# An encoder trunk on one core: SSD decay sums by triangle matmuls instead of scans over rows from DRAM, with a new interleaving

## The chip, the cores and the metric

The kernel runs on one core of one Trainium2 chip. The metric is the device time of one execution in microseconds; the time before is the median of three runs. The engines are TensorE (PE, with its weight loads PEld as a second track), VectorE (DVE), ScalarE (ACT), GpSimd (POOL) and SyncE (SP), which issues most DMAs and waits in order like the others.

## The reference

Two post-norm layers over 512 positions of width 1024. Each layer mixes with two head groups side by side and then runs an MLP:

```python
mix = concat([y_ssd, y_s5], -1) @ w_out
h = layer_norm(ALPHA * h + mix)
h = layer_norm(ALPHA * h + square(relu(h @ w1)) @ w2)
```

The SSD group has 16 heads, two directions and chunks of 128 positions. Its decay matrix, per head, direction and chunk, is what the change touches:

```python
Adt  = dt * A                               # one row of 512 per head and direction
Lmat = exp(_segsum(Adt))                    # exp of sums of Adt over (s, t], lower triangle
CB   = einsum('bclgn,bcsgn->bgcls', Cc, Bc)
y_diag = einsum('bgcls,bgrcls,bcsgrp->bclgrp', CB, Lmat, X)
```

The S5 group has 64 channel groups, each with a complex diagonal state, a forward and a backward scan, a gelu and a gated projection.

## The kernel before

All matrix products of weights are done as three fp32r matmuls (`mm3`: high part by high, high by low, low by high). For each weight tile, ACT writes the high part `whi` and DVE the low part `wlo`. Other products are plain fp32 and go through TensorE as two instructions each.

A layer is a mixer and an MLP. The mixer merges two generators. `ssd_group` runs for four groups; each has a convolution for B and for C, the products `cb_ps` with two masks (`CBU`, `CBLo`), and then two channel tiles of two heads each, 16 heads in all. `s5_stream` first makes the input states (tables `Wv`, matmuls `v_ps`), then 62 steps of a scan (three small DVE operations `sc`, `sc`, `cur` and an ACT copy each), then for m = 0 to 7 an output table `Wy` (DVE), its small products `kk_ps`, and the output matmuls `y` with `gT` transposes. In layer 0 the `Wv` and `Wy` tables are computed in the mixer; those of layer 1 are computed beforehand, during the MLP of layer 0 (`s5_tables`, drawn on by the string `gen`), and are loaded.

`KN["mrg"]` says how many S5 steps are drawn before each SSD step, `lag` how many tiles the input states trail, `po` which pieces get an offset in priority. The instructions' order on each engine is then set by a scheduler at build time. What is left of the S5 stream after the last SSD step is emitted ahead of the output projection of the SSD half (`rows_proj(A["wo"][l, 0], ...)`, matmuls `rp`), and the scheduler may mix the two. Then comes the gated projection `glu_ps`.

For one head, before: a DMA `ab` spreads two rows of Adt (one per direction, the first or last element of each chunk made -1e30 by two small operations in `dt_prep`) over 128 partitions. One scan adds along t and restarts at each chunk's diagonal by a maximum with the constant `md`; a second runs backward from the first's result; ACT takes the exponential:

```python
V.tensor_tensor_scan(E2, ab[:, 0], C("md"), NEG, op0=ALU.add, op1=ALU.max)
V.tensor_tensor_scan(E[:, ::-1], ab[:, 1][:, ::-1], E2[:, ::-1], NEG, op0=ALU.add, op1=ALU.max)
S.activation(E, E, AF.Exp)
```

The tile `ab` has one buffer, E has two. E is multiplied by the weighted mask products `w` and used in `y_ps` (L632); `eb` rows, also from DRAM, feed the terms between chunks (L635, L638). PSUM tags: `mm` three banks, `ss` one, `sm` two (`Xrow_ps`, `Brow_ps`, `cb_ps`, `st_ps`), `s5` two.

Of the kernel before, what the change touches and what calls it, by code (L numbers as in the profile page):

```python
# [10 lines left out]
F32 = mybir.dt.float32  # L11
F32R = mybir.dt.float32r
I32 = mybir.dt.int32
AF = mybir.ActivationFunctionType
# [27 lines left out]


KN = dict(
    mrg=[[5, 0, 1, 0, 3, 0, 3, 5, 0, 10, 1, 3, 0, 9, 4, 0, 0, 0, 1, 0,
# [3 lines left out]
    pt0=3, lag=[2, 5], vb=(3, 2), gvb=(3, 2), cbb=2, wyb=4, raw=2, whi=3, wlo=3,  # L49
    nb=dict(mm=3, ss=1, sm=2, s5=2),  # L50
    po=[{"dt": 60, "z": 30, "v": 60, "w": 150, "scan": 300}, {"w": -30, "dt": 150, "scan": 30}], curb=2,
    gen="112122220000021030201011",
)


# [1 line left out]
def kernel(ctx: ExitStack, tc: tile.TileContext, A, out, depth=L):  # L57
# [19 lines left out]
    def C(n):  # L77
        a, b = CST[n]
        return cst[:, a:b]
# [209 lines left out]
    def dt_prep(l, pool, hT, prm):  # L289
        wd = pool.tile([128, 8, 32], F32, tag="wd", name="wd", bufs=1)  # L290
        nc.sync.dma_start(wd, A["wd"][l])
        p = psum("sm", "dtp")
        for k in range(8):
            for i in range(2):
                for c in range(4):
                    PE.matmul(p[32 * c:32 * c + 32, 0:128], lhsT=wd[:, k],
                              rhs=hT[i][:, k, c * 128:(c + 1) * 128].bitcast(F32),
                              start=(k == 0 and i == 0), stop=(k == 7 and i == 1),
                              tile_position=(0, 32 * c))

        def t(nm, n=128):
            return pool.tile([128, n], F32, tag="dt_" + nm, name="dt_" + nm, bufs=1)
        v, e, z, z2, q, dt = t("v"), t("e"), t("z"), t("z2"), t("q"), t("dt")
        V.tensor_scalar(v, p[:, 0:128], prm["P"]("dtb"), None, op0=ALU.add)
        V.scalar_tensor_tensor(e, v, -1.0, v, op0=ALU.mult, op1=ALU.max)
        S.activation(e, e, AF.Exp, scale=-1.0)
        V.tensor_scalar(z, e, 2.0, None, op0=ALU.add)
        V.reciprocal(out=z, in_=z)
        V.tensor_tensor(z, z, e, op=ALU.mult)
        V.tensor_tensor(z2, z, z, op=ALU.mult)  # L310
        V.tensor_scalar(q, z2, 1.0 / 17, None, op0=ALU.mult)
        for c in (15, 13, 11, 9, 7, 5, 3):
            V.scalar_tensor_tensor(q, q, 1.0 / c, z2, op0=ALU.add, op1=ALU.mult)
        V.scalar_tensor_tensor(q, q, 1.0, z, op0=ALU.add, op1=ALU.mult)
        V.tensor_scalar(v, v, 0.0, None, op0=ALU.max)
        V.scalar_tensor_tensor(dt, q, 2.0, v, op0=ALU.mult, op1=ALU.add)
        aef = pool.tile([128, 2, 128], F32, tag="dt_aef", name="dt_aef", bufs=1)
        a, ef = aef[:, 0], aef[:, 1]
        V.tensor_scalar(a, dt, prm["A"], None, op0=ALU.mult)
        Pp, Rp, one = t("P", 129), t("R", 129), C("ones")  # L320
        V.memset(Pp[:, 0:1], 0.0)
        V.memset(Rp[:, 128:129], 0.0)
        V.tensor_tensor_scan(Pp[:, 1:129], one, a, 0.0, op0=ALU.mult, op1=ALU.add)
        V.tensor_tensor_scan(Rp[:, 0:128][:, ::-1], one, a[:, ::-1], 0.0, op0=ALU.mult, op1=ALU.add)
        dec, tot = z, t("tot", 1)
        isf, isb = C("isf"), C("isb")
        V.tensor_scalar(ef, Pp[:, 1:129], isf, None, op0=ALU.mult)
        V.scalar_tensor_tensor(ef, Rp[:, 0:128], isb, ef, op0=ALU.mult, op1=ALU.add)
        V.tensor_scalar(dec, Rp[:, 1:129], isf, None, op0=ALU.mult)
        V.scalar_tensor_tensor(dec, Pp[:, 0:128], isb, dec, op0=ALU.mult, op1=ALU.add)  # L330
        S.activation(ef, ef, AF.Exp)
        S.activation(dec, dec, AF.Exp)
        S.activation(tot, Pp[:, 128:129], AF.Exp)
        V.tensor_tensor(dec, dec, dt, op=ALU.mult)
        for i, c in ((0, isf), (127, isb)):
            V.tensor_scalar(a[:, i:i + 1], c, NEG, a[:, i:i + 1], op0=ALU.mult, op1=ALU.add)
        ad = dr.tile([2, 16, 2, 4, 128], F32, tag="ad", name="ad", bufs=2)
        for c in range(4):
            nc.sync.dma_start(ad[:, :, :, c].rearrange("d h i s -> (d h) i s"), aef[32 * c:32 * c + 32])
        p = psum("sm", "dtT")  # L340
        PE.transpose(p[:, 0:128], dt, ident)
        PE.transpose(p[:, 128:256], dec, ident)
        tb = q
        V.tensor_scalar(tb, one, tot, None, op0=ALU.mult)
        PE.matmul(p[:, 256:384], lhsT=tb, rhs=ident, start=True, stop=True)
        fac = per.tile([128, 3, 4, 2, 16], F32, tag="fac", name="fac", bufs=1)
        S.activation(fac.rearrange("p a c d h -> p (a c d h)"), p[:, 0:384], AF.Copy)
        return dict(ad=ad, dtT=fac[:, 0], dec=fac[:, 1], tot=fac[:, 2])


    def s5_u(us, o, Ud, m):
# [209 lines left out]
    def ssd_group(l, pool, act, prm, dtp, g, yd, ys):  # L561
# [16 lines left out]
        for j in range(2):  # L578
# [27 lines left out]
            for h in range(2):  # L606
                hh = 2 * ct + h
                E = pool.tile([128, T], F32, tag="E", name="E", bufs=2)
                E2 = pool.tile([128, T], F32, tag="tmp", name="E2", bufs=3)
                ab = pool.tile([128, 2, T], F32, tag="ab", name="ab", bufs=1)  # L610
                eb = pool.tile([128, 2, 384], F32, tag="eb", name="eb", bufs=2)
                nc.sync.dma_start(ab, dtp["ad"][:, hh, 0].rearrange("d c s -> d (c s)").unsqueeze(0).to_broadcast(
                    [128, 2, T]))
                for dd in range(2):
                    nc.sync.dma_start(eb[:, dd], dtp["ad"][dd, hh, 1, 1 - dd:4 - dd].rearrange(
                        "c s -> (c s)").unsqueeze(0).to_broadcast([128, 384]))
                V.tensor_tensor_scan(E2, ab[:, 0], C("md"), NEG, op0=ALU.add, op1=ALU.max)
                V.tensor_tensor_scan(E[:, ::-1], ab[:, 1][:, ::-1], E2[:, ::-1], NEG, op0=ALU.add, op1=ALU.max)
                S.activation(E, E, AF.Exp)
                w = pool.tile([128, 4, 128], F32, tag="w", name="w", bufs=1)  # L620
                w2 = pool.tile([128, 4, 128], F32, tag="tmp", name="w2", bufs=3)
                for c in range(4):
                    S.activation(w[:, c], CB[0][:, c], AF.Copy, scale=dtp["dtT"][:, c, 0, hh:hh + 1])
                    S.activation(w2[:, c], CB[1][:, c], AF.Copy, scale=dtp["dtT"][:, c, 1, hh:hh + 1])
                V.tensor_tensor(w, w, w2, op=ALU.add)
                Ev = E.rearrange("p (c n) -> p c n", c=4)
                V.tensor_tensor(Ev, Ev, w, op=ALU.mult)
                V.tensor_tensor(eb[:, 0], CT[:, 128:512], eb[:, 0], op=ALU.mult)
                V.tensor_tensor(eb[:, 1], CT[:, 0:384], eb[:, 1], op=ALU.mult)
                for c in range(4):  # L630
                    o = yp[64 * h:64 * h + 64, c * 128:(c + 1) * 128]
                    PE.matmul(o, lhsT=X[:, c, 64 * h:64 * h + 64], rhs=E[:, c * 128:(c + 1) * 128],  # L632
                              start=True, stop=False, tile_position=(0, 64 * h))
                    if c > 0:
                        PE.matmul(o, lhsT=St[0][:, c - 1, 64 * h:64 * h + 64], rhs=eb[:, 0, (c - 1) * 128:c * 128],  # L635
                                  start=False, stop=(c == 3), tile_position=(0, 64 * h))
                    if c < 3:
                        PE.matmul(o, lhsT=St[1][:, c, 64 * h:64 * h + 64], rhs=eb[:, 1, c * 128:(c + 1) * 128],  # L638
                                  start=False, stop=True, tile_position=(0, 64 * h))
                yield  # L640
# [304 lines left out]
def prepare(inp):  # L945
# [66 lines left out]
    cput("id", s == t)  # L1012
    cput("U", t >= s)
    cput("Lo", t <= s)
    cput("md", np.where(np.tile(t == s, (1, 4)), 0.0, 2 * NEG))
    cput("i16", (s % 16) == np.arange(16)[None])
    isf = ((s // 16) % 2 == 0)
    cput("isf", isf)
# [20 lines left out]
```

## Time and profile before

| | |
|---|---|
| median of the runs shown | 1901.4 us (1901.06 to 1903.05) |
| the profiled execution, its own time | 1897.68 us |
| its span | 1895.7 us |
| busy: PE, PEld, DVE, ACT, POOL | 1711.2, 1398.3, 1307.6, 778.1, 73.7 us |
| mean granted TensorE clock | 0.951 |
| DMA | 275.68 MB, mean 145 GB/s |

Busy times are unions over an engine's instructions; a busy PE counts a matmul's latency too. Layer 0's mixer takes about 60 to 537 us, its MLP up to about 1035, layer 1's mixer 1035 to 1430, its MLP the rest. The granted clock is told as a share of full speed (1.0 is 2.4 GHz, 0.5 is 1.2 GHz).

### The profile page before, as it was taken

The numbers are of one execution on the slowest core, as the hardware profiler recorded it, in microseconds if no ns is written. First come the engines' busy times: TensorE is split into PE (matmuls) and PEld (weight loads), VectorE is DVE, ScalarE is ACT, GpSimd is POOL, SyncE is SP. The second block draws the span as 40 slices with busy tenths as digits, with TensorE's granted clock in tenths as the row PEclk, the third lists the DMA queues.
The fourth block names the chain that finished last, engine by engine and source line by source line (L and its number), as shares of the span: only waits on it lengthen the run. The fifth ranks groups of instructions, "written<-read, shape, count | busy, mean of one in ns | idle before, by whom it ended". The sixth has DMA issues, their size and how long they took to land.

```text
span 1895.7 us, 27446 instructions
## 1 busy us (share of the span) xinstructions
PE 1711.2 (90%) x10872; PEld 1398.3 (74%) x10872; DVE 1307.6 (69%) x2176; ACT 778.1 (41%) x1305; POOL 73.7 (4%) x99
## 2 busy tenths in 40 slices
PE   4989888687799999999999999875989999999998
PEld 3767666575578877778888887665767888888886
DVE  7789989997646889994446679999614663434345
ACT  3356556742143433223233466657314332323231
POOL 1000000000000101110001000000000010000001
PEclk8999899788799999999999999887999999999999
DMA  5887444244324188763335784432683422333232
GB/s 191 238 217 200 114 116 138 73 156 117 103 98 133 62 263 278 260 217 108 101 123 168 228 263 130 123 100 73 207 236 123 126 75 89 101 98 96 83 101 89
DMA packets 120864, 275.68 MB, mean 145 GB/s; under 512 B 11424, under 2 KB 55456, under 8 KB 120096
## 3 DMA queue, kind: packets, MB, share of 16 engines
q1 hardware_dynamic: 113248, 247.85, 43.7%
q0 software_dynamic: 7488, 26.09, 3.7%
q8 instruction: 85, 1.39, 0.3%
q14 instruction: 43, 0.35, 0.1%
HBM read 237.06 MB, written 36.83 MB: 144 GB/s over the span
## 4 chain that ended last, share of the span: by engine, by line
PE 64%; DVE 19%; DMA 9%; issue 4%; ACT 4%; POOL 0%; POOLq 0%; SPq 0%; DVEq 0%; ACTq 0%
PE rp L105 8%; PE rp L106 8%; PE rp L104 8%; PE up_ps L104 5%; PE up_ps L105 5%; PE up_ps L106 5%; PE y L518 3%; DVE wlo L94 3%; DMA ab<-ad 2%; PE glu_ps L104 2%; PE glu_ps L105 2%; PE glu_ps L106 1%; PE xbc_ps L104 1%; DMA Bv<-in_bb 1%; PE xbc_ps L105 1%
## 5 line engine op out<-in xcount | busy, mean ns | idle before, releaser
L94 DVE TENSOR_TENSOR wlo<-raw,whi 128x1024 fp32r<-128x1024 f32 x224 | 273.4, 1221 | 302.0 <-ACT whi L93 298.4
L93 ACT ACTIVATE whi<-raw 128x1024 fp32r<-128x1024 f32 x224 | 237.4, 1060 | 511.0 <-PE up_ps L105 189.7
L104 PE MATMUL up_ps<-hThi,whi 128*128 128x512 f32 (+1 forms) x560 | 208.7, 375 | 3.3 <-DVE hr L907 3.0
L105 PE MATMUL up_ps<-hTlo,whi 128*128 128x512 f32 (+1 forms) x560 | 209.0, 374 | 0.1
L106 PE MATMUL up_ps<-hThi,wlo 128*128 128x512 f32 (+1 forms) x560 | 208.7, 373 | 0.0
L105 PE MATMUL rp<-wlo,ahi 128*128 128x512 f32 x448 | 176.8, 395 | 0.4 <-DVE wlo L94 0.4
L106 PE MATMUL rp<-whi,alo 128*128 128x512 f32 x448 | 176.6, 395 | 0.0
L104 PE MATMUL rp<-whi,ahi 128*128 128x512 f32 x448 | 165.5, 397 | 0.9 <-ACT whi L93 0.9
L104 PE MATMUL xbc_ps<-hThi,whi 128*128 128x512 f32 x256 | 106.6, 416 | 18.1 <-DVE xbc L548 14.6
L104 PEld LDWEIGHTS up_ps<-hThi,whi 128*128 128x128 f32 x560 | 105.4, 189 | 23.7 <-issue 2.2
L105 PEld LDWEIGHTS up_ps<-hTlo,whi 128*128 128x128 f32 x560 | 105.9, 189 | 18.9 <-issue 0.4
L106 PEld LDWEIGHTS up_ps<-hThi,wlo 128*128 128x128 f32 x560 | 105.8, 189 | 18.7 <-issue 0.2
L106 PE MATMUL xbc_ps<-hThi,wlo 128*128 128x512 f32 x256 | 104.3, 408 | 0.0
L105 PE MATMUL xbc_ps<-hTlo,whi 128*128 128x512 f32 x256 | 104.1, 407 | 0.0
L104 PEld LDWEIGHTS rp<-whi,ahi 128*128 128x128 f32 x448 | 83.9, 188 | 21.6 <-ACT whi L93 1.6
L106 PEld LDWEIGHTS rp<-whi,alo 128*128 128x128 f32 x448 | 84.1, 188 | 21.0 <-issue 0.4
L105 PEld LDWEIGHTS rp<-wlo,ahi 128*128 128x128 f32 x448 | 84.1, 188 | 20.8 <-DVE wlo L94 0.7
L419 ACT ACTIVATE XV<-cur 128x128 f32<-128x128 f32 x124 | 52.6, 428 | 88.3 <-DVE cur L418 88.2
L518 PE MATMUL y<-Wy,XV 64*64 64x128 f32 x1024 | 80.1, 300 | 0.0
L917 DVE TENSOR_TENSOR h<-h,rp 128x512 f32<-128x512 f32 x64 | 43.4, 682 | 49.2 <-PE rp L106 49.2
L104 PEld LDWEIGHTS xbc_ps<-hThi,whi 128*128 128x128 f32 x256 | 50.8, 198 | 31.2 <-DVE xbc L548 13.1
L518 PEld LDWEIGHTS y<-Wy,XV 64*64 64x64 f32 x1024 | 62.6, 147 | 13.3 <-issue 13.2
(278 smaller groups left out, 3711.2 us busy)
## 6 DMA issues: line engine op xcount, KB each, us to landing
raw<-in_w SPq DMA_DIRECT2D x128, 512.0 KB, 3.6
raw<-in_wi SPq DMA_DIRECT2D x64, 512.0 KB, 4.2
Pv<-pd SPq DMA_DIRECT2D x32, 512.0 KB, 6.3
ab<-ad SPq DMA_DIRECT2D x32, 512.0 KB, 5.4
raw<-in_wo SPq DMA_DIRECT2D x32, 512.0 KB, 3.6
eb<-ad SPq DMA_DIRECT2D x64, 192.0 KB, 4.4
Bv<-in_bb SPq DMA_DIRECT2D x16, 512.0 KB, 5.3
U<-Ud SPq DMA_DIRECT2D x16, 512.0 KB, 5.8
```

Source lines behind the costliest of these rows:

```text
L93: S.activation(hi, raw, AF.Copy)
L94: V.tensor_tensor(lo, raw, hi.bitcast(F32), op=ALU.subtract)
L104: PE.matmul(o, lhsT=sh, rhs=mh, start=first, stop=False)
L105: PE.matmul(o, lhsT=sh, rhs=ml, start=False, stop=False)
L106: PE.matmul(o, lhsT=sl, rhs=mh, start=False, stop=last)
L419: S.activation(x1, new, AF.Copy)
L518: PE.matmul(yv[64 * a:64 * a + 64, q], lhsT=XV[64 * a:64 * a + 64, ri, 4 * m + q, 64 * dd:64 * dd + 64], rhs=W[dd][64 * a:64 * a + 64, ri, ...
L917: V.tensor_tensor(hs, hs, o, op=ALU.add)
```

## The change

Per head, the rows `ab`, both scans and the constant `md` go. One DVE product R is made, 128 partitions (s) by two directions, four chunks and 128 columns: the two triangle masks U and Lo, times Adt as a column (`aT`, taken from a fourth transpose in `dt_prep`). Two fp32 matmuls with strict triangles `Ls` and `Us` sum it into one PSUM bank `D_ps` of the tag `sm`, and ACT takes the exponential from there. DRAM rows `ad` hold only the `ef` half, for `eb`. The tables of interleaving, lags, offsets and `gen` are new, and the two pieces R and `y` are given offsets of their own.

```diff
-       "isf": (912, 913), "isb": (913, 914), "ones": (914, 1042)}
+CST = {"id": (0, 128), "U": (128, 256), "Lo": (256, 384), "Ls": (384, 512), "Us": (512, 640), "i16": (640, 656),
...
-    pt0=3, lag=[2, 5], vb=(3, 2), gvb=(3, 2), cbb=2, wyb=4, raw=2, whi=3, wlo=3,
+    pt0=3, lag=[1, 3], vb=(3, 2), gvb=(3, 2), cbb=2, wyb=4, raw=2, whi=3, wlo=3,
...
-    po=[{"dt": 60, "z": 30, "v": 60, "w": 150, "scan": 300}, {"w": -30, "dt": 150, "scan": 30}], curb=2,
-    gen="112122220000021030201011",
+    po=[{"z": 30, "v": 60, "w": 150, "scan": -300, "R": -100, "y": -30}, {"w": 300, "dt": 60, "scan": 30, "z": -150, "R": -100}],
+    curb=2, Dt="sm", gen="111002220201202202023020",
...
-        for i, c in ((0, isf), (127, isb)):
-            V.tensor_scalar(a[:, i:i + 1], c, NEG, a[:, i:i + 1], op0=ALU.mult, op1=ALU.add)
-        ad = dr.tile([2, 16, 2, 4, 128], F32, tag="ad", name="ad", bufs=2)
+        ad = dr.tile([2, 16, 4, 128], F32, tag="ad", name="ad", bufs=2)
...
-        fac = per.tile([128, 3, 4, 2, 16], F32, tag="fac", name="fac", bufs=1)
-        S.activation(fac.rearrange("p a c d h -> p (a c d h)"), p[:, 0:384], AF.Copy)
+        PE.transpose(p[:, 384:512], a, ident)
+        fac = per.tile([128, 4, 4, 2, 16], F32, tag="fac", name="fac", bufs=1)
+        S.activation(fac.rearrange("p a c d h -> p (a c d h)"), p, AF.Copy)
...
-                nc.sync.dma_start(ab, dtp["ad"][:, hh, 0].rearrange("d c s -> d (c s)").unsqueeze(0).to_broadcast(
-                    [128, 2, T]))
...
-                V.tensor_tensor_scan(E2, ab[:, 0], C("md"), NEG, op0=ALU.add, op1=ALU.max)
-                V.tensor_tensor_scan(E[:, ::-1], ab[:, 1][:, ::-1], E2[:, ::-1], NEG, op0=ALU.add, op1=ALU.max)
-                S.activation(E, E, AF.Exp)
+
+                with prio("R"):
+                    V.tensor_tensor(R, cst[:, 128:384].rearrange("p (d t) -> p d t", d=2).unsqueeze(2).to_broadcast(
+                        [128, 2, 4, 128]), dtp["aT"][:, :, :, hh].rearrange("p c d -> p d c").unsqueeze(3).to_broadcast(
+                        [128, 2, 4, 128]), op=ALU.mult)
+                    Dp = psum(KN["Dt"], "D_ps")
+                    for dd, nm in enumerate(("Ls", "Us")):
+                        PE.matmul(Dp, lhsT=C(nm), rhs=R[:, dd].rearrange("p c t -> p (c t)"), start=(dd == 0), stop=(dd == 1))
+                    S.activation(E, Dp, AF.Exp)
```

The first place is DVE in layer 0, behind the products of the last head. Before, the scan of the S5 stream (`sc`, `cur`) still runs there, between the splits of the output projection's weights; 34 of its 62 steps stand ahead of the last head:

```order
L662 TENSOR_TENSOR ssq<-ssq,xbc 128x512
L414 TENSOR_TENSOR sc_2133<-cur,l_287 128x256
L94 TENSOR_TENSOR wlo<-raw,whi 128x1024
L417 TENSOR_TENSOR sc_2134<-sc_2133,XV 128x128
L418 TENSOR_TENSOR cur<-sc_2134,sc_2133 128x128
L414 TENSOR_TENSOR sc_2140<-cur,l_287 128x256
L94 TENSOR_TENSOR wlo<-raw,whi 128x1024
```

In the changed kernel all 62 steps stand ahead of the last head's R (L613), and the `Wy` tables follow it at once:

```order
L415 TENSOR_TENSOR cur<-sc_2316,sc_2315 128x128
L596 SCALAR_TENSOR_TENSOR S<-S,fac,st_ps 128x64 x4
L613 TENSOR_TENSOR R<-cst,fac 128x1024
L627 TENSOR_TENSOR E<-E,w 128x512
L625 TENSOR_TENSOR w<-w,w_4169 128x512
L457 TENSOR_TENSOR Wy<-cp,pw_257 128x1024 x2
L459 TENSOR_TENSOR Wy<-Wy,tw 128x1024
L458 TENSOR_TENSOR tw<-cp,pw_257 128x1024
```

So 28 scan steps moved from behind the last head to ahead of it. In both kernels 4 of the 16 `Wy` tables of layer 0 (two for each m) stand ahead of the last head and 12 behind it.

The second place is TensorE in layer 0 behind the heads. Before, the 192 matmuls `rp` of the output projection stand together, and then each m's products `kk_ps` and outputs `y` (names with numbers) follow without any `rp` between them:

```order
L518 MATMUL y_2809<-Wy,XV 64x128 x8
L529 MATMUL gT_ps<-cst,gs 128x128 x8
L467 MATMUL kk_ps<-Wy,cb 32x128 x16
L473 MATMUL kk_ps<-cp,cb 32x16 x16
L513 MATMUL y_3379<-Gt,U 64x128 x2
```

In the changed kernel the `rp` matmuls are spread between them:

```order
L103 MATMUL rp_4478<-whi,hThi 128x512
L104 MATMUL rp_4478<-wlo,hThi 128x512
L464 MATMUL kk_ps<-Wy,cb 32x128 x16
L470 MATMUL kk_ps<-cp,cb 32x16 x16
L510 MATMUL y_3755<-Gt,U 64x128 x2
L515 MATMUL y_3755<-Wy,XV 64x128 x8
L510 MATMUL y_3755<-Gt,U 64x128 x2
```

The outputs `y` of m = 0 and 1 now even stand ahead of the last head's `y_ps`, and six m follow.

The third place is TensorE in layer 1, at the last heads. Before, the gate's projection, the state products and the head's own matmuls follow one another; all but four of the 320 `y` matmuls stand behind the heads:

```order
L106 MATMUL z_ps<-hThi,wlo 128x512
L592 MATMUL st_ps<-xd,Brow 128x128 x3
L632 MATMUL y_ps<-E,Xrow 64x128
L592 MATMUL st_ps<-xd,Brow 128x128 x3
L555 MATMUL Xrow_ps<-cst,xbc 128x128 x4
```

In the changed kernel the `y` matmuls stand around the state products and the new pairs `D_ps`, and 240 of the 320 stand ahead of the first `rp`:

```order
L589 MATMUL st_ps<-xd,Brow 128x128 x3
L515 MATMUL y_11641<-Wy,XV 64x128 x3
L618 MATMUL D_ps<-R,cst 128x512 x2
L515 MATMUL y_11641<-Wy,XV 64x128 x2
L510 MATMUL y_11641<-Gt,U 64x128 x2
L515 MATMUL y_11641<-Wy,XV 64x128 x8
L103 MATMUL z_ps<-hThi,whi 128x512
```

So outputs of six m moved from behind the heads to between the last ones, and each head has two matmuls more, in the order in which TensorE takes them.

## Rows read from the trace of the kernel before

**Rows 1.** The profile page, its first line: the span.

```profile
span 1895.7 us, 27446 instructions
```

**Rows 2.** Windows: each row a stretch, with the columns of the first line.

```profile
core 0: us, PE busy (x) PEld busy (x) DVE busy (x) ACT busy (x) POOL busy (x), PEclk, DMA share, GB/s
60.00:537.00 477.00, 385.92 (x3210) 310.77 (x3208) 397.19 (x699) 222.91 (x427) 11.53 (x18) 0.89 0.51 143
110.90:375.70 264.80, 217.63 (x1444) 176.90 (x1442) 247.39 (x443) 161.25 (x317) 2.00 (x3) 0.92 0.51 141
375.70:537.00 161.30, 125.67 (x1293) 98.37 (x1292) 109.93 (x199) 43.84 (x83) 7.74 (x13) 0.84 0.40 120
440.00:520.00 80.00, 55.84 (x854) 41.89 (x850) 50.76 (x70) 9.28 (x23) 5.46 (x10) 0.80 0.42 117
1035.00:1430.00 395.00, 344.05 (x2620) 281.94 (x2620) 278.02 (x541) 211.35 (x398) 7.18 (x10) 0.92 0.59 172
1198.20:1318.00 119.80, 91.39 (x470) 75.74 (x470) 109.19 (x225) 81.17 (x164) 0.00 (x0) 0.84 0.36 99
1318.00:1330.00 12.00, 6.11 (x38) 5.87 (x38) 10.47 (x26) 6.43 (x11) 0.00 (x0) 0.59 0.23 65
```

**Rows 3.** Groups by line and form: busy us, mean ns, idle before and its releaser.

```profile
L618 DVE TENSOR_TENSOR_SCAN E<-ab,E 128x512 f32<-128x512 f32 x32 | 39.0, 1219 | 3.9 <-PE y_ps L632 3.8
L617 DVE TENSOR_TENSOR_SCAN E<-ab,cst 128x512 f32<-128x512 f32 x32 | 39.0, 1219 | 8.3 <-DMA ab<-ad 8.2
...
L460 DVE TENSOR_TENSOR Wy<-cp,pw 128x1024 f32<-128x1024 f32 x32 | 38.4, 1217 | 8.3 <-PE y L518 8.3
```

**Rows 4.** Groups by line, VectorE, 375.7 to 537 us: the scan's three operations.

```profile
L414 DVE TENSOR_TENSOR sc<-cur,l 128x256 f32<-128x256 f32 x27 | 11.5, 424 | 0.7
L417 DVE TENSOR_TENSOR sc<-sc,XV 128x128 f32<-128x128 f32 x27 | 10.5, 388 | 0.6
L418 DVE TENSOR_TENSOR cur<-sc,sc 128x128 f32<-128x128 f32 x28 | 8.1, 291 | 1.6
```

**Rows 5.** The tile ab: idle time until its rows landed, and its time to landing.

```profile
  DMA ab<-ad: 8.2, 8
...
DMA to landing us min/median/max: 4.6/5.4/10.1
```

**Rows 6.** Timeline of TensorE at three places: start us, us, engine, line, operation.

```profile
282.01 0.38 PE L638 MATMUL y_ps<-eb,S 128*64 128x128 f32 x2
282.23 0.38 PE L632 MATMUL y_ps<-E,Xrow 128*64 128x128 f32 x2
...
289.21 0.39 PE L105 MATMUL z_ps<-hTlo,whi 128*128 128x512 f32 x1
289.44 0.39 PE L106 MATMUL z_ps<-hThi,wlo 128*128 128x512 f32 x1
...
1358.16 1.09 PE L518 MATMUL y<-Wy,XV 64*64 64x128 f32 x16
...
1359.55 1.09 PE L518 MATMUL y<-Wy,XV 64*64 64x128 f32 x16
```

**Rows 7.** Timeline of VectorE: the first tables of m = 2 and of m = 4.

```profile
442.67 2.36 DVE L460 TENSOR_TENSOR Wy<-cp,pw 128x1024 f32<-128x1024 f32 x2 [1.92 <-PE y L518]
...
470.89 2.36 DVE L460 TENSOR_TENSOR Wy<-cp,pw 128x1024 f32<-128x1024 f32 x2 [1.92 <-PE y L518]
```

**Rows 8.** Groups by line, TensorE, 60 to 537 us, three that waited.

```profile
L104 PE MATMUL z_ps<-hThi,whi 128*128 128x512 f32 x64 | 26.3, 411 | 6.2 <-DVE xbc L548 6.2
...
L638 PE MATMUL y_ps<-eb,S 128*64 128x128 f32 x96 | 21.7, 313 | 9.6 <-DVE S L599 9.6
...
L467 PE MATMUL kk_ps<-Wy,cb 128*32 128x128 f32 x256 | 15.9, 348 | 25.5 <-DVE Wy L462 25.5
```

**Rows 9.** Timeline, ScalarE and VectorE: the factors' copy, the first head's first scan.

```profile
101.92 0.49 ACT L347 ACTIVATE fac<-dtT 128x384 f32<-128x384 f32 x1
...
110.88 1.23 DVE L617 TENSOR_TENSOR_SCAN E<-ab,cst 128x512 f32<-128x512 f32 x1 [0.23 <-DMA ab<-ad]
```

More of the change, by code (lines that the diff above doesn't have):

```diff
@@ L31 @@
 C3 = float(np.float32(2 * math.pi - C1 - C2))
-CST = {"id": (0, 128), "U": (128, 256), "Lo": (256, 384), "md": (384, 896), "i16": (896, 912),
-       "isf": (912, 913), "isb": (913, 914), "ones": (914, 1042)}
-NCST = 1042
-NEG = -1e30
+CST = {"id": (0, 128), "U": (128, 256), "Lo": (256, 384), "Ls": (384, 512), "Us": (512, 640), "i16": (640, 656),
+       "isf": (656, 657), "isb": (657, 658), "ones": (658, 786)}
+NCST = 786
 SP = {"cw": (0, 80), "cb": (80, 96), "dtb": (96, 97), "alog": (97, 98), "D": (98, 106), "nw": (106, 114),
@@ L44 @@
 KN = dict(
-    mrg=[[5, 0, 1, 0, 3, 0, 3, 5, 0, 10, 1, 3, 0, 9, 4, 0, 0, 0, 1, 0,
+    mrg=[[5, 0, 1, 0, 3, 0, 3, 5, 0, 11, 0, 3, 0, 9, 4, 0, 0, 0, 1, 0,
           2, 0, 0, 0, 0, 0, 0, 0, 0, 0, 1, 0, 0, 0, 0, 0, 1, 2, 0, 1],
[2 rows of a table removed]
-    pt0=3, lag=[2, 5], vb=(3, 2), gvb=(3, 2), cbb=2, wyb=4, raw=2, whi=3, wlo=3,
[2 rows of a table added]
+    pt0=3, lag=[1, 3], vb=(3, 2), gvb=(3, 2), cbb=2, wyb=4, raw=2, whi=3, wlo=3,
     nb=dict(mm=3, ss=1, sm=2, s5=2),
-    po=[{"dt": 60, "z": 30, "v": 60, "w": 150, "scan": 300}, {"w": -30, "dt": 150, "scan": 30}], curb=2,
-    gen="112122220000021030201011",
+    po=[{"z": 30, "v": 60, "w": 150, "scan": -300, "R": -100, "y": -30}, {"w": 300, "dt": 60, "scan": 30, "z": -150, "R": -100}],
+    curb=2, Dt="sm", gen="111002220201202202023020",
 )
@@ L316, in dt_prep @@
         V.scalar_tensor_tensor(dt, q, 2.0, v, op0=ALU.mult, op1=ALU.add)
-        aef = pool.tile([128, 2, 128], F32, tag="dt_aef", name="dt_aef", bufs=1)
-        a, ef = aef[:, 0], aef[:, 1]
+        a, ef = t("a"), t("ef")
         V.tensor_scalar(a, dt, prm["A"], None, op0=ALU.mult)
@@ L334, in dt_prep @@
         V.tensor_tensor(dec, dec, dt, op=ALU.mult)
-        for i, c in ((0, isf), (127, isb)):
-            V.tensor_scalar(a[:, i:i + 1], c, NEG, a[:, i:i + 1], op0=ALU.mult, op1=ALU.add)
-        ad = dr.tile([2, 16, 2, 4, 128], F32, tag="ad", name="ad", bufs=2)
+        ad = dr.tile([2, 16, 4, 128], F32, tag="ad", name="ad", bufs=2)
         for c in range(4):
-            nc.sync.dma_start(ad[:, :, :, c].rearrange("d h i s -> (d h) i s"), aef[32 * c:32 * c + 32])
+            nc.sync.dma_start(ad[:, :, c].rearrange("d h s -> (d h) s"), ef[32 * c:32 * c + 32])
         p = psum("sm", "dtT")
@@ L345, in dt_prep @@
         PE.matmul(p[:, 256:384], lhsT=tb, rhs=ident, start=True, stop=True)
-        fac = per.tile([128, 3, 4, 2, 16], F32, tag="fac", name="fac", bufs=1)
-        S.activation(fac.rearrange("p a c d h -> p (a c d h)"), p[:, 0:384], AF.Copy)
-        return dict(ad=ad, dtT=fac[:, 0], dec=fac[:, 1], tot=fac[:, 2])
+        PE.transpose(p[:, 384:512], a, ident)
+        fac = per.tile([128, 4, 4, 2, 16], F32, tag="fac", name="fac", bufs=1)
+        S.activation(fac.rearrange("p a c d h -> p (a c d h)"), p, AF.Copy)
+        return dict(ad=ad, dtT=fac[:, 0], dec=fac[:, 1], tot=fac[:, 2], aT=fac[:, 3])
     def s5_u(us, o, Ud, m):
@@ L608, in ssd_group @@
                 E = pool.tile([128, T], F32, tag="E", name="E", bufs=2)
-                E2 = pool.tile([128, T], F32, tag="tmp", name="E2", bufs=3)
-                ab = pool.tile([128, 2, T], F32, tag="ab", name="ab", bufs=1)
+                R = pool.tile([128, 2, 4, 128], F32, tag="R", name="R", bufs=1)
                 eb = pool.tile([128, 2, 384], F32, tag="eb", name="eb", bufs=2)
-                nc.sync.dma_start(ab, dtp["ad"][:, hh, 0].rearrange("d c s -> d (c s)").unsqueeze(0).to_broadcast(
-                    [128, 2, T]))
                 for dd in range(2):
-                    nc.sync.dma_start(eb[:, dd], dtp["ad"][dd, hh, 1, 1 - dd:4 - dd].rearrange(
+                    nc.sync.dma_start(eb[:, dd], dtp["ad"][dd, hh, 1 - dd:4 - dd].rearrange(
                         "c s -> (c s)").unsqueeze(0).to_broadcast([128, 384]))
-                V.tensor_tensor_scan(E2, ab[:, 0], C("md"), NEG, op0=ALU.add, op1=ALU.max)
-                V.tensor_tensor_scan(E[:, ::-1], ab[:, 1][:, ::-1], E2[:, ::-1], NEG, op0=ALU.add, op1=ALU.max)
-                S.activation(E, E, AF.Exp)
+                with prio("R"):
[6 more added lines that the diff above has]
+                    S.activation(E, Dp, AF.Exp)
                 w = pool.tile([128, 4, 128], F32, tag="w", name="w", bufs=1)
@@ L1014, in prepare @@
     cput("Lo", t <= s)
-    cput("md", np.where(np.tile(t == s, (1, 4)), 0.0, 2 * NEG))
+    cput("Ls", t < s)
+    cput("Us", t > s)
     cput("i16", (s % 16) == np.arange(16)[None])
```

4 rows, old and new, of the table mrg are left out of this document.

## Prediction

> **What bounds the kernel now.** I read the page first: the profiled execution spans 1895.7 us [rows 1], 2.0 us less than its own time of 1897.7. Then the windows, stage by stage. The two mixers take 477 and 395 us, with TensorE busy 385.9 and 344.1 [rows 2]. Taken from the page's totals (1711.2 busy), this leaves 981.2 busy of 1023.7 us for the rest, 96%: there TensorE is full, the change leaves the work alone, and only the mixers matter. The reader should see that in neither is one engine the bound throughout. From the first head's scan to the last head's (110.9 to 375.7 us), VectorE is busy 247.4 of 264.8 us, 93%, and TensorE 217.6, 82%. Behind the last head of layer 0 (375.7 to 537), neither is full: TensorE 125.7 and VectorE 109.9 of 161.3 us. The worst part is 440 to 520, with TensorE at 55.8 and VectorE at 50.8 of 80 us, at a mean granted clock of 0.80. There the tables run as a chain: from one even m to the next even one 28.2 us pass, 14.1 for each m [rows 7], and TensorE waits for the tables, 25.5 us over the mixer [rows 8]. In layer 1, 28.4 of TensorE's 51 idle us lie at 1198 to 1318 and 5.9 at 1318 to 1330 [rows 2].
>
> **What the change costs and saves on each engine.** Per head two scans of 1.219 us go [rows 3]. R, a product of 128x1024 fp32 with both inputs spread, is not in the trace; L460 has that size, type and spread inputs, 1.217 us [rows 3]. The net is 1.22 us of VectorE per head: 32 x 1.22 = 39 us in all, 19.5 a layer.
>
> The two matmuls of 512 columns in fp32 are not in the trace either. Each is two instructions. Two instructions of 128 fp32 columns follow the next such pair at 0.22 us (282.01 to 282.23), so four times that, 0.88, is one end; 512 columns in the reduced form advance in 0.23 us (289.21 to 289.44), so two of them, 0.46, is the other [rows 6]. I take 0.88, the row with the same type: 1.76 us a head, 28 us a layer, 56 in all; the low end is 29 in all. The Trainium skill, "FP8 and Floating Point Precision" (TensorE Precision Notes), says that true fp32 takes four passes through the array. By that rule a matmul would cost four of the 0.23 us steps, 0.91, and all of them 58 us, which speaks against the change: TensorE, the busier engine, gets more work than VectorE loses. The trace agrees so far that fp32 advances about four times slower per column than the reduced form.
>
> The DMA `ab` goes: 32 transfers of 5.4 us median to landing; VectorE sat idle for it 8.2 us in all [rows 5], since other work covers most. I count nothing for the rest. The exponential reads PSUM instead of SBUF; the fourth transpose and the two small operations less in `dt_prep` are under a microsecond a layer: nothing. SP's queue loses 32 issues; no wait read here is for a weight load behind them, so nothing. Bank `sm` gets 32 more users; I cover that by a rival. The new `gen` shuffles tables under a TensorE that is busy nearly throughout in the MLP of layer 0: zero, give or take 3 us.
>
> **Layer 0, three stretches.** *To the first head.* The first scan waited for `ab` until 110.88; R needs the factors, copied by 102.4 [rows 9]: up to -8 us. I take -8, with 0 as the other end.
>
> *Heads.* 15 heads lie here: 15 x 1.22 = -18.3 of VectorE. But 28 scan steps come in from behind the last head: the three operations are busy 30.1 us there in 27 to 28 rounds [rows 4], 1.1 a step, so +30.8. VectorE's work is 247.4 + 30.8 - 18.3 = 259.9; at the same 93% this takes 279 us in place of 265: +14. TensorE has 217.6 + 26 = 244, still under it (88%).
>
> *Behind the last head.* The scan is gone from it, and `rp` stands between the tables' products, so that TensorE's wait for the tables is filled with `rp`, which stood alone before. TensorE's work at full clock is at least 125.7 x 0.84 = 106 us; less one m's outputs, which move ahead (four times the 1.39 us from 1358.16 to 1359.55 [rows 6], 5.6), plus two pairs, 3.5: 104. How full can it be? Now it is busy 78% of this stretch. At 78% the stretch takes 133 us (-28), at 95% 109 (-52). The chain of six m takes 6 x 14.1 = 85 us and is no longer the whole of it, so I take 85%: 122 us, -39.
>
> Together -8 + 14 - 39 = -33.
>
> **Layer 1.** 28 us of `D_ps` come in. Against that stand TensorE's 51 idle us: outputs of six m, 6 x 5.6 = 33 us, now stand between the last heads, where 34 us were idle, and the slow clock there (0.84, 0.59 [rows 2]) should rise with fewer holes. If 28 of the 51 are filled, nothing changes; if 51 are and the clock gives 9 back (half of 0.16 x 120), -32. VectorE's 278 us do not bind. I take 43 filled: -15. The wait for the factors lies under `u_ps` matmuls here: nothing.
>
> Sum: -33 - 15 = -48 on the execution's 1897.7, 1849.7. The median of the runs shown is 3.7 above that execution, so I forecast 1853 us.
>
> **Rivals.** *Smaller: TensorE is too full to give it back.* If `rp` only moves TensorE's idle time about (78%, -28), R is no earlier (0) and heads cost +14, layer 0 gives -14; in layer 1 the added 28 us fill just the holes (0). 1897.7 - 14 + 3.7 = 1887 us. For it: 82% and 87% are TensorE's shares already, at in-order waits that stay. Against: the tables' wait of 25.5 us is one that `rp` can plainly fill.
>
> *Larger: both mixers fill up.* 95% behind layer 0's last head (-52 in place of -39, so -46) and layer 1's -32: 1897.7 - 78 + 3.7 = 1823 us. For it: the holes come with a clock of 0.59 to 0.84, so filling them pays twice. The Trainium skill, "TensorE: Matmul & The Clock Gate" (Part 1), says that an idle array is throttled to half rate and that activity releases it. By that rule this rival gains; the trace agrees, with 0.59 in the emptiest stretch against 0.92 in the heads of layer 0. Against: VectorE then has to run at well over 93% as well.
>
> *Slower: TensorE stops at the pairs.* TensorE takes its instructions in order. A pair waits for R, which stands in VectorE's queue, for the one buffer of R, and for one of two banks `sm`, which is held until VectorE has finished a chain of `S` or ACT its exponential. Behind it stand projections and the other heads' products. Such waits exist: 9.6 us in all for `S`, 6.2 us for a convolution [rows 8]. At 1.5 us a head that nothing else covers (48/32) the gain is gone; at 2.2 the time is 1901 + 22 = 1923. For it: three users of `sm` per channel tile become five. Against: E has two buffers and R can run a head ahead, and the old chain (landing, two scans) was longer than R and a pair.
>
> **Chances and range.** The forecast 0.50, its own range 1835 to 1873; smaller 0.25, of which 0.04 lies within 0.2% (3.8 us) of the median, about what a measurement of this kernel can tell from no change; larger 0.13; slower 0.12. Faster is 0.50 + 0.21 + 0.13 = 0.84, the same 0.04, slower 0.12. The range leaves out the slower case and the last part of the larger one: 1826 to 1893.
>
> **What the profile would show.** R near 1.22 us, and a pair ending about 1.9 us behind its start; no DMA `ab`; VectorE busy about 39 us less in all, TensorE 30 to 56 more. In layer 0 the last head comes a little later than 376 us, but `glu_ps` starts near 503 in place of 537; layer 1's mixer takes about 380 us. Wrong would be: a mean above 1.5 us of wait at `D_ps` or at what stands behind it; `kk_ps` still waiting 20 us or more for `Wy`; or layer 1's mixer at 395 us or longer, with TensorE idle at the pairs.

## The result, and the profile after

The changed kernel takes 1884.3 us (median; 1877.2 to 1884.6) against 1902.2 us (1901.1 to 1905.8) for the kernel before: 0.9897 times, 95% interval 0.9872 to 0.9922. A second comparison gave 0.9899 (0.9881 to 0.9917). So it is faster by 1.0%, about 20 us by these ratios (18 between the two medians); the forecast was 2.5%, 48 us.

The profiled execution's page, first the span, then the busy time of each engine with its share and instructions:

```profile
span 1882.6 us, 27592 instructions
...
PE 1751.7 (93%) x11002; PEld 1410.5 (75%) x11002; DVE 1276.6 (68%) x2140; ACT 773.0 (41%) x1300; POOL 74.4 (4%) x99
```

TensorE is busy 40.5 us more than before and VectorE 31.0 less. Taken by themselves, the new operations cost what the forecast gave them; the totals move by less than its 56 and 39 us, TensorE's at a mean granted clock of 0.966 in place of 0.951. The instructions on the tile R (duration in ns, least/median/most, then first and last start), and TensorE's timeline at one pair:

```profile
L618 PE MATMUL D_ps<-R,cst x128: 590/592/1192, 143.3 to 1351.0; 128*128 128x512 f32 x128
L613 DVE TENSOR_TENSOR R<-cst,fac x32: 1216/1224/1236, 97.2 to 1348.3; 128x1024 f32<-128x1024 f32 x32
```

```profile
1174.94 1.88 PE L618 MATMUL D_ps<-R,cst 128*128 128x512 f32 x4
1176.25 0.80 PE L104 MATMUL xbc_ps<-hTlo,whi 128*128 128x512 f32 x1
1176.89 0.40 PE L105 MATMUL xbc_ps<-hThi,wlo 128*128 128x512 f32 x1
1177.12 0.39 PE L103 MATMUL xbc_ps<-hThi,whi 128*128 128x512 f32 x1
```

R takes 1.22 us. Behind the pair the matmuls follow at 0.23 us again (1176.89 to 1177.12); take one such step off the 1.95 us from 1174.94 to 1176.89, and the pair's four instructions have 1.72 us, against 1.76 in the sum.

The windows that answer to [rows 2]: the heads of layer 0 from the first R to the last, what lies behind them up to `glu_ps`, layer 1's mixer, and in it the heads:

```profile
core 0: us, PE busy (x) PEld busy (x) DVE busy (x) ACT busy (x) POOL busy (x), PEclk, DMA share, GB/s
97.20:404.30 307.10, 256.48 (x1609) 196.87 (x1607) 271.56 (x529) 171.91 (x349) 2.89 (x4) 0.89 0.39 102
404.30:529.50 125.20, 113.43 (x1296) 88.06 (x1295) 75.32 (x105) 32.63 (x55) 9.82 (x13) 0.97 0.50 148
1027.70:1425.80 398.10, 374.39 (x2760) 295.28 (x2760) 265.65 (x529) 215.27 (x407) 6.99 (x10) 0.96 0.53 152
1049.60:1348.30 298.70, 276.20 (x1880) 216.42 (x1875) 221.18 (x457) 179.04 (x352) 2.88 (x4) 0.95 0.47 127
```

Two of the three stretches went otherwise than forecast. Behind the last head TensorE is now busy 91% of 125 us, in place of 78% of 161, at a granted clock of 0.97 in place of 0.84. In the heads of layer 0 VectorE is busy 88% where it was 93%, and TensorE 84%. In layer 1's heads TensorE is at 92% and VectorE at 74%: there the fuller engine is TensorE.

Cut at five places (the start of the last head's R or first scan in layer 0; the first `glu_ps`; the first `dtp` of layer 1; layer 1's first `glu_ps`; the end), the profiled executions give this, in us:

| | to the last head | to `glu_ps` | to layer 1 | its mixer | rest | span |
|---|---|---|---|---|---|---|
| before | 375.6 | 161.4 | 498.2 | 402.7 | 457.8 | 1895.7 |
| changed | 404.3 | 125.2 | 498.2 | 398.1 | 456.8 | 1882.6 |
| changed, second profile | 399.8 | 125.2 | 500.0 | 393.8 | 456.8 | 1875.6 |

So 36 us come back behind the heads of layer 0, 24 to 29 of them are lost in these heads, and layer 1 gives 5 to 9. (Layer 1's mixer is counted from its first `dtp` here, some 8 us longer than the 395 of [rows 2].)

What waits now (total us, times, longest), VectorE first, then TensorE:

```profile
DVE eb L628 <- DMA eb<-ad: 29.4, 18, 5.9
...
DVE R L613 <- PE D_ps L618: 15.7, 10, 6.8
...
DVE eb L629 <- DMA eb<-ad: 7.3, 8, 1.9
...
DVE E L627 <- ACT E L619: 5.7, 8, 1.6
```

```profile
PE st_ps L589 <- DVE xd L584: 24.1, 10, 4.2
PE D_ps L618 <- DVE S L596: 14.4, 4, 4.3
...
PE kk_ps L464 <- DVE Wy L459: 8.1, 5, 2.3
```

TensorE's wait for the tables is down from 25.5 us [rows 8] to 8.1. Two waits are new on VectorE: at R, whose one buffer the pair of the head before has yet to read, and for the `eb` rows, 36.7 us in its two lines. In the kernel before, those two lines hold 3.1:

```profile
DVE eb L629 <- DMA eb<-ad: 1.8, 4, 0.8
...
DVE eb L628 <- DMA eb<-ad: 1.3, 3, 0.6
```

### The profile page after: what moved, and what is told of

Its sections match the earlier page's. It is cut to its first block, busy times and chain, and to the rows that moved or that the text cites. A ratio compares the mean times of both kernels' runs of the same rounds, so it can differ in the third digit from the quotient of the medians.

```text
span 1882.6 us, 27592 instructions
## 1 busy us (share of the span) xinstructions
PE 1751.7 (93%) x11002; PEld 1410.5 (75%) x11002; DVE 1276.6 (68%) x2140; ACT 773.0 (41%) x1300; POOL 74.4 (4%) x99
## 4 chain that ended last, share of the span: by engine, by line
PE 58%; issue 19%; DVE 11%; DMA 9%; ACT 2%; SPq 1%; POOL 0%; POOLq 0%; DVEq 0%; ACTq 0%
PE rp L103 8%; PE rp L104 8%; PE rp L105 8%; PE up_ps L103 6%; PE up_ps L104 6%; PE up_ps L105 6%; PE glu_ps L104 2%; PE glu_ps L103 2%; PE glu_ps L105 2%; DVE wlo L93 2%; DMA eb<-ad 2%; PE D_ps L618 1%; PE y L515 1%; DMA U<-Ud 1%; DMA Ud<-us 1%
## 5 line engine op out<-in xcount | busy, mean ns | idle before, releaser
L618 PE MATMUL D_ps<-R,cst 128*128 128x512 f32 x128 | 71.4, 671 | 16.5 <-DVE S L596 14.4
L515 PE MATMUL y<-Wy,XV 64*64 64x128 f32 x1024 | 76.2, 284 | 0.0
```

Source lines behind the costliest of these rows:

```text
L515: PE.matmul(yv[64 * a:64 * a + 64, q], lhsT=XV[64 * a:64 * a + 64, ri, 4 * m + q, 64 * dd:64 * dd + 64], rhs=W[dd][64 * a:64 * a + 64, ri, ...
L618: PE.matmul(Dp, lhsT=C(nm), rhs=R[:, dd].rearrange("p c t -> p (c t)"), start=(dd == 0), stop=(dd == 1))
```

## The experiments

Two theories stood at first. **A:** the interleaving gives the gain, and the operations cancel. **B:** the operations give it, and the tables only fit them. Two more came up: that the landing of `eb` took the place of that of `ab`, and that TensorE's added 56 us are paid in full.

**The change in halves, and two suspects.** e1 has the changed operations with all tables of before, e2 before's operations with all new tables. e3 issues each pair twice, with the same result. e4 leaves the 64 `eb` loads out, so the terms between chunks are not the reference's.

```diff
+                    for rep in range(2):
+                        for dd, nm in enumerate(("Ls", "Us")):
+                            PE.matmul(Dp, lhsT=C(nm), rhs=R[:, dd].rearrange("p c t -> p (c t)"), start=(dd == 0), stop=(dd == 1))
```

```diff
-                    nc.sync.dma_start(eb[:, dd], dtp["ad"][dd, hh, 1 - dd:4 - dd].rearrange(
-                        "c s -> (c s)").unsqueeze(0).to_broadcast([128, 384]))
...
-                V.tensor_tensor(eb[:, 0], CT[:, 128:512], eb[:, 0], op=ALU.mult)
+                V.tensor_tensor(eb[:, 0], CT[:, 128:512], cst[:, 128:512], op=ALU.mult)
```

> The changed kernel with the tables of before (mrg, lag, po, gen): only the operations change. Theory A (the gain of 1.0% comes mostly from the new interleaving, which shortens the stretch behind layer 0's last head, and the operations alone give about nothing, since the rows eb are then waited for and TensorE gets 56 us more): 1892 to 1910 us, ratio to before 0.995 to 1.005. Theory B (the operations give the gain and the tables only fit it): 1877 to 1890 us.

> The kernel before with the new tables: only the interleaving changes, with scans and DMA ab. Theory A: the short stretch behind layer 0's last head appears here too, but VectorE has 1.22 us more per head ahead of it and no TensorE time is added: 1875 to 1895 us. Theory B: the new tables without the new operations are no better than the old ones: 1900 to 1925 us.

> The changed kernel with each pair of triangle matmuls issued twice into the same bank (same result): TensorE gets about 56 us more again. If TensorE is the bound of both mixers by now (it is busy 404 of 470 and 375 of 399 us): 40 to 55 us slower, 1925 to 1940. If VectorE's queue and its waits set the heads' stretch: 10 to 30 us slower, 1895 to 1915.

> The changed kernel with the 64 DMAs eb left out; the products that used them read constants instead, so the terms between chunks are not those of the reference. If the landing of eb (36.7 us of VectorE waiting in the changed kernel against 3 to 5 before) took the place of the wait for ab: 15 to 35 us faster than the changed kernel, 1850 to 1870. If TensorE's added work is what ate the gain: within 8 us of it, 1876 to 1888.

Ratios to before: e1 0.9973 (0.9961 to 0.9985), e2 1.0121 (1.0105 to 1.0138), e3 1.0225 (1.0209 to 1.0241), e4 0.9887 (0.9868 to 0.9905). The operations alone give 5 us, the tables alone cost 23; neither A nor B is right, only both together give 20. Without the loads of `eb` the time is the same within about 2 us, though VectorE waited 36.7 us for them. That speaks against `eb` as the main cause, but does not settle it: e4's order was set anew too (next step), and its last head of layer 0 comes at 390.5 us, where the changed kernel has 400 to 404. The doubled pair costs 62 us for some 55 of TensorE, which spoke for the full price.

**Less of the pair, more of the product.** So taking TensorE's work off should give time back. e5 drops the second matmul of each pair (and with it half of the decay sums), e6 runs the pair in the reduced fp32 form (R and a copy `tri` of the triangles of type `F32R`, one instruction a matmul), e7 forms R twice; a0 is the changed kernel beside them.

```diff
+    tri = per.tile([128, 2, 128], F32R, tag="tri", name="tri")
...
-                R = pool.tile([128, 2, 4, 128], F32, tag="R", name="R", bufs=1)
+                R = pool.tile([128, 2, 4, 128], F32R, tag="R", name="R", bufs=1)
...
-                        PE.matmul(Dp, lhsT=C(nm), rhs=R[:, dd].rearrange("p c t -> p (c t)"), start=(dd == 0), stop=(dd == 1))
+                        PE.matmul(Dp, lhsT=tri[:, dd], rhs=R[:, dd].rearrange("p c t -> p (c t)"), start=(dd == 0), stop=(dd == 1))
...
+    S.activation(tri.rearrange("p d t -> p (d t)"), cst[:, 384:640], AF.Copy)
```

> The changed kernel itself, in the same call as the runs beside it, so that they can be compared: about 1884 us, ratio to the kernel before near 0.990.

> Leaves out the second matmul of each pair, and with it the backward half of the decay sums; TensorE loses 32 x 0.88 = 28 us. If TensorE's added time costs its full price, as the doubled pair suggested (+62 us for about +56), the time falls by 20 to 28 us, to 1856 to 1864. If the pair only costs when it is added beyond what the holes can take (the forecast's own idea, 43 of 51 idle us filled), taking half of it away leaves holes: at most 8 us less, 1876 or more.

> The two matmuls of a pair run in the reduced fp32 form, one instruction each: R and a copy of the two triangles are of that type, so the products are rounded to it. TensorE loses about 32 x 1.3 = 42 us. At TensorE's full price 1840 to 1855 us; if VectorE or the order of the two binds now, 1870 or more.

> The product R is formed twice, with the same result: VectorE gets 32 x 1.22 = 39 us more, TensorE nothing. If only TensorE binds, 0 to 10 us more (1884 to 1894). If the two engines take turns in a fixed order, so that work of either lengthens the path, 20 to 40 us more (1904 to 1924).

a0 0.9899, e5 0.9900 (0.9874 to 0.9926), e6 0.9906 (0.9891 to 0.9920), e7 1.0198 (1.0176 to 1.0220). Work taken off TensorE gives nothing, and 39 us more on VectorE cost 57. Taken at their word, these say that VectorE is the bound and e3 that TensorE is: they can't be read together. An edit of a few instructions makes the scheduler set others anew: lined up by their start in the traces, some 730 to 780 of the changed kernel's 2,140 VectorE instructions stand elsewhere in e3, e5, e6 and e7 (670 in e4), where the edits themselves add or take away 32 to 128 instructions.

**The same edits with the order held.** So the order of the changed kernel was read out and laid on the edited ones: from each instruction of an engine to the next an order-only edge, SP's DMAs and GpSimd's among them, an added instruction right behind its twin.

```diff
+def keep_order(tc, nc):
...
+            if prev is not None:
+                tc.add_manual_dep(prog[i], prev.name, info, reason="keep_order")
+            prev = prog[i]
...
+        keep_order(tc, nc)
```

In the traces of g3 and g4 the instructions of all four engines stand in the changed kernel's order one by one, the added ones apart. The held order with nothing edited was not timed; g8 (below), which adds only a buffer, comes nearest, with 0.9906. g1 puts before's operations into it (the first scan, here written in place into `ab`, stands where R stood, the second behind it; each `ab` load but a layer's first is issued behind the first scan of the head before, since there is one buffer). g2, g3 and g4 are the edits of e6, e7 and e3.

> Before's operations (two scans from rows loaded from DRAM, no pair) with every other instruction of the four engines and of SP's queue held in exactly the order of the changed kernel; the first scan stands where R stood, the second behind it. VectorE has 39 us more than the changed kernel, TensorE 56 us less. If TensorE's added time is what ate the gain: 20 to 50 us less than the changed kernel, 1830 to 1860. If VectorE's time sets the heads: 20 to 40 us more, 1900 to 1920. If the order is what decides and the operations are about worth each other: within 8 us of the changed kernel.

> As e6_pair_in_reduced_form (each matmul of a pair one instruction in reduced form, TensorE about 42 us less), but with the order of the changed kernel held, so that nothing else moves. TensorE at its full price: 1840 to 1858. If the pair lies beside VectorE's work in this order: at most 8 us less, 1870 to 1880.

> As e7_product_twice (VectorE 39 us more), with the order of the changed kernel held and the second product right behind the first. If VectorE sets the heads: 25 to 45 us more than the changed kernel. If TensorE does, and the +58 us of e7 came from the new order: 10 us or less.

> As e3_double_pair (TensorE 56 us more), with the order of the changed kernel held. TensorE at its full price: 45 to 60 us more than the changed kernel. If the pair lies beside VectorE's work and the +62 us of e3 came from the new order: 20 us or less.

> As e5_half_of_each_pair (the second matmul of each pair, and with it the backward half of the decay sums, left out; TensorE 28 us less), with the order of the changed kernel held. By the price that g2 showed for TensorE's time taken off (15 us for 42, 0.37): 10 us less than the changed kernel, ratio about 0.985. By the price that g4 showed for time added (45 for 56, 0.8): 22 us less, about 0.978.

g5, run after these, is e5 with the order held. Ratio to before, and the difference to the changed kernel (ratio less 0.9898, times 1897 us):

| | added on | ratio (95%) | us to changed |
|---|---|---|---|
| g2, pair in reduced form | TensorE -40 | 0.9816 (0.9798 to 0.9833) | -16 |
| g5, half of each pair | TensorE -28 | 0.9816 (0.9790 to 0.9842) | -16 |
| g4, pair twice | TensorE +55 | 1.0133 (1.0113 to 1.0152) | +45 |
| g3, product twice | VectorE +39 | 0.9968 (0.9952 to 0.9984) | +13 |
| g1, before's operations | VectorE +39, TensorE -55, `ab` back | 1.0142 (1.0125 to 1.0159) | +46 |

The -40 of g2 is from its timeline, where a pair holds TensorE 0.46 us in place of 1.72:

```profile
1124.69 0.63 PE L619 MATMUL D_ps<-R,tri 128*128 128x512 f32 x2
1125.15 0.39 PE L106 MATMUL xbc_ps<-hThi,wlo 128*128 128x512 f32 x1
```

By the intervals, each of these differences is uncertain by 4 to 6 us. Now the runs agree with each other: TensorE's time has a price of 0.8 us a microsecond when added and 0.56 for the first 28 us taken off (16/28); for the next 12 none is seen, though up to 6 us would be within the uncertainty. e5 and e6 had lost the same 16 us to a new order (behind the last head of layer 0 they take 143 and 145 us, the changed kernel 125), e7 44 us more than g3, e3 17 more than g4. The windows show the price stage by stage. g2, the heads of layer 0 and layer 1's mixer:

```profile
95.90:391.50 295.60, 236.02 (x1559) 192.25 (x1559) 270.97 (x529) 169.24 (x347) 2.89 (x4) 0.89 0.40 107
...
1013.20:1401.90 388.70, 357.06 (x2728) 291.65 (x2728) 265.42 (x529) 214.75 (x408) 6.99 (x10) 0.96 0.53 155
```

g4, the same two:

```profile
95.30:421.60 326.30, 277.45 (x1645) 204.49 (x1647) 271.31 (x530) 172.04 (x347) 2.89 (x4) 0.92 0.37 97
...
1043.50:1461.40 417.90, 396.08 (x2825) 303.44 (x2825) 266.73 (x529) 216.12 (x408) 6.99 (x10) 0.98 0.50 144
```

g3, the same two:

```profile
97.10:408.80 311.70, 257.42 (x1603) 196.95 (x1603) 289.69 (x545) 171.89 (x346) 2.88 (x4) 0.89 0.38 102
...
1033.80:1429.90 396.10, 371.19 (x2760) 292.74 (x2760) 284.60 (x545) 215.90 (x408) 6.99 (x10) 0.97 0.53 152
```

VectorE's work in the heads of layer 0 is 271 us in g2, the changed kernel and g4 alike, but it is spread over 295.6, 307.1 and 326.3 us: 92%, 88% and 83% busy, by the length of a pair that is on another engine. With the short pair VectorE is back near its share of before. g5's pair is nearly twice as long as g2's, and its heads end at 392.0 us, its mixer of layer 1 takes 390.0, as good as g2's 391.5 and 388.7. In layer 1 the product twice adds 19 us to VectorE and leaves the mixer where it was (396.1 against 394 to 398), while the pair twice adds 20 to 24: there, by one profile of each, TensorE alone is paid. In the heads of layer 0 both are: with the product twice VectorE is busy 289.7 us, and they end at 408.8.

g1 shows what the order and the operations are worth apart: with before's operations in the new order the stretch behind the last head is 127 us as well, so the 36 us gained there are the order's. The tables alone don't make that order: in e2, where the scheduler was free, the stretch takes 166.9 us. But in g1 the heads of layer 0 end at 423.6, 48 us later than before, and layer 1's mixer takes 420.1. Its heads of layer 0, its tile `ab`, and two of TensorE's waits:

```profile
105.40:423.60 318.20, 235.01 (x1488) 192.66 (x1490) 288.10 (x543) 167.00 (x340) 2.89 (x4) 0.83 0.44 119
```

```profile
  DMA ab<-ad: 26.6, 6
...
DMA to landing us min/median/max: 4.6/5.3/9.3
```

```profile
PE y_ps L631 <- DVE E L626: 38.4, 16, 7.0
...
PE v_ps L397 <- DVE Wv L380: 18.0, 2, 17.8
```

VectorE stands 26.6 us for `ab`, where it stood 8.2 [rows 5], and TensorE 38.4 us for the exponential's product. VectorE's 39 us more cost only 13 in g3, so most of g1's 46 is left to such waits, in an order that was not made for rows from DRAM; one wait of 17.8 us for a table of the S5 stream is among them, and the granted clock in these heads is 0.83, in the changed kernel's 0.89. That is argued from the rows; no run takes it apart.

**Where TensorE's time reaches VectorE.** The wait at R grows from 15.7 us to 54.0 in g4 and falls to 4.8 in g2. If R's one buffer is the cause, a second one is worth those waits; there is room for it in layer 1. g8 is the changed kernel with it, g9 is g4, g10 is g2.

```diff
-                R = pool.tile([128, 2, 4, 128], F32, tag="R", name="R", bufs=1)
+                R = pool.tile([128, 2, 4, 128], F32, tag="R", name="R", bufs=1 + l)
```

> The changed kernel with a second buffer for R in layer 1 alone, the order of all instructions held. In the changed kernel VectorE stands 10.7 us of layer 1 (and 5.1 of layer 0) at R until the pair of the head before has read the one buffer. If that wait is how TensorE's time reaches the path, layer 1's mixer gets 7 to 11 us shorter and layer 0 stays: ratio about 0.985. If TensorE's own time is the price, within 3 us of the changed kernel.

> g4 (each pair issued twice) with the second buffer for R in layer 1 alone, order held. In g4 VectorE stands 31.5 us of layer 1 at R, and that mixer takes 418 us against 394 to 398. By the buffer's theory layer 1's mixer falls to about 400 and the kernel gains 15 to 20 us on g4, ratio about 1.004; by TensorE's own time it stays within 5 us of g4, 1.013.

> g2 (pair in the reduced form) with the second buffer for R in layer 1 alone, order held. Only 4.7 us of waiting at R are left in g2, so by the buffer's theory 2 to 5 us less than g2, ratio 0.979 to 0.981; by TensorE's own time no change, 0.982.

g8 0.9906 (0.9888 to 0.9924), g9 1.0127 (1.0108 to 1.0145), g10 0.9822 (0.9794 to 0.9850): no change in any of them. The theory of the buffer falls. In both profiles the wait at R in layer 1 is gone (10.7 us in the changed kernel, 31.5 in g4), but VectorE's waits from 1030 us on now hold this, in g8:

```profile
DVE E L627 <- ACT E L619: 12.1, 7, 6.4
```

and in g9:

```profile
DVE eb L629 <- DMA eb<-ad: 27.7, 11, 6.0
DVE E L628 <- ACT E L620: 21.4, 11, 7.1
```

The waits at E were 3.6 us in layer 1 of the changed kernel and 2.4 in g4, the one for `eb` 19.2 in g4. VectorE now forms R in time and stands one step later, where it multiplies the exponential of the same pair. What is late is the pair itself in TensorE's queue; the buffer only said where VectorE noticed.

**VectorE's time taken off.** g6 forms R on GpSimd (`G.tensor_tensor` for `V.tensor_tensor`), g7 with g2's reduced pair too, the order held.

> The product R is formed on GpSimd instead of VectorE, with the order of the changed kernel held: VectorE has 39 us less. If VectorE's time taken off has the price that g3 showed for time added (0.33): 13 us less than the changed kernel, ratio about 0.983. If the heads wait for TensorE alone: no gain. No run has shown such a product on GpSimd; if it takes over 5 us there or slows VectorE beside it, the kernel gets slower.

> The reduced form of g2 and the product on GpSimd of g6 together, order held: TensorE 42 us less and VectorE 39 us less. If both engines share the path in turns, the two gains add up (15 + 13): about 1851 us, ratio near 0.975. If one of them was the bound, the larger gain alone: about 1864.

g6 0.9929 (0.9909 to 0.9949), g7 0.9926 (0.9906 to 0.9947): both about 6 us slower than the changed kernel, little more than the uncertainty. They don't answer the question, because VectorE didn't get its 39 us back: it is busy 1277.0 us in g6, with 32 instructions less. Two rows of g6 show why:

```profile
L613 POOL TENSOR_TENSOR R<-cst,fac x32: 1904/1918/2394, 95.2 to 1351.1; 128x1024 f32<-128x1024 f32 x32
```

```profile
L627 DVE TENSOR_TENSOR E<-E,w x32: 671/684/2054, 147.9 to 1355.8; 128x512 f32<-128x512 f32 x32
```

In the changed kernel the longest of these 32 products takes 696 ns. So the price of VectorE's time taken off stays open.

Of the kernels that leave nothing out, g2 is the fastest, and g10 the same within the noise: g2 takes 1863.9 us (1860.7 to 1864.8), 0.9816 (0.9798 to 0.9833) times the kernel before, with the decay sums formed from rounded inputs.

## Why the prediction was too large

**Right.** R (1.22) and the pair (1.72 against 1.76) were sized as they came out. *Behind the last head*: 122 us were forecast, 125.2 measured, -36 in place of -39, with `rp` between the tables as forecast, and `kk_ps` waits 8.1 us, under the bound of 20. That the number is so near is in part luck: TensorE is busy 113.4 us where 104 were counted, but 91% of the stretch in place of 85%. The granted clock there rose from 0.84 to 0.97 as TensorE's share rose from 78% to 91%. The Trainium skill ("TensorE: Matmul & The Clock Gate", Part 1) says that activity releases the throttle on the clock; the trace agrees. TensorE's wait at `D_ps` is 16.4 us in all, and 24.1 at `st_ps` behind it (6.0 before): under 1.5 us a head, so the slower rival, by its own mark, did not come. The MLP of layer 0 and the rest moved by at most 2 us.

**Wrong, first: the pair's time was counted as covered.** In the heads of layer 0 the step was "TensorE has 217.6 + 26 = 244, still under it (88%)", with VectorE "at the same 93%". VectorE's work was near enough, but its share was no constant: it fell to 88% as TensorE's filled. g2 puts a figure on it: with the short pair the heads end at 391.5 (394.1 in g10) in place of 399 to 404 (399.1 in g8), 5 to 13 us. In layer 1 the step was "I take 43 filled", -15. Measured is -5 to -9; TensorE is busy 374.4 of 398.1 us (94%), where 380 us would have asked for 98%. Before, on the same cut, it was this:

```profile
1035.20:1437.90 402.70, 349.81 (x2695) 286.36 (x2694) 277.82 (x542) 213.59 (x403) 7.18 (x10) 0.92 0.58 171
```

So its idle time fell from 52.9 to 23.7 us: some 29 were filled, about the 28 that came in. With the short pair the mixer gets 14.0 us shorter than before, the forecast's term, but with 20 us less of pair than the forecast counted. By the medians the pair's price is 16 us over both layers, over half of the 28 that are missing.

**Wrong, second: the earlier first head.** "I take -8": R did come 13.6 us before the old first scan (97.2 against 110.9 [rows 9]), but its pair starts only at 143.3, and VectorE's work in the heads is 271.6 us in place of 259.9, ahead of them 73.8 in place of 83.6. Work that had stood ahead of the first scan now stands behind the first R; nothing was saved, some 8 us of the 28. With 0 for this term the heads' forecast is 389.7, and g2 has 391.5. Why the first pair stands that late was not tried, nor, with the order held, what the waits for `eb` cost in these heads.

**Wrong, third: `ab` at nothing.** This erred the other way inside a larger sum. The landing was 8.2 us of VectorE's waits before, in before's own order; in the new order it is 26.6, and TensorE waits behind it. The operations and the tables are not two gains to be added (-5 and +23), and the forecast had no term for what they are worth to each other.

Of the rivals, "smaller" has the time (1887) and in layer 1 the mechanism: the added 28 us fill about the holes. Behind the heads it was wrong, since TensorE got nearly full there; its 14 us of heads were 24 to 29 instead. "Larger" came near in that one stretch's share (95% forecast, 91% measured), but not in its time (-52, and -36 measured).

## What to carry to other kernels

- Where two engines are each busy 82 to 93% of a stretch and wait for one another in order, neither has to be the bound: here a microsecond of TensorE cost some 0.6 to 0.8 (none was seen for the last 12 us taken off) and one of VectorE, added, a third, so an operation moved from one to the other is costed on both, and a share of 93% is not kept once the other engine fills up.
- An edit under a scheduler tests the edit and a new order at once. Here the new order alone was worth 16 to 44 us, as much as the whole effect; with the order held, the four edits that had contradicted each other agreed. e4 was not repeated so, and its answer is the weaker for it.
- A wait says where an engine notices, not what is late: when a second buffer took it away, VectorE waited as much a step or two further on, and the time was the same.

## What the runs showed of the hardware that was not expected

GpSimd needs 1.92 us for the product that takes VectorE 1.22, and beside it single VectorE instructions get longer: E's products above last 2054 ns at most in place of 696, and over the whole trace of g6, compared one by one with the changed kernel's, 28 instructions take 37 us longer, none by more than 1.72. So VectorE's busy time doesn't fall at all (1277.0 against 1276.6 us). The Trainium skill ("SBUF — State Buffer", Terms) says that the two engines share a port pair under an exclusive lock that is held for the full instruction. The trace agrees: no instruction is lengthened by more than one such product.

A matmul of 512 fp32 columns takes 0.86 us in its two instructions (half of 1.72), one in the reduced form 0.23 (half of 0.46): close to four times as much.
